# Element-wise sums moved from GpSimd to VectorE, and a gentler packing rule for buffers

## The chip, the cores and the metric

The kernel runs on one core of a Trainium2 chip. The metric is the device time of one execution in microseconds (us), the median of three runs. The engines have short names: PE is TensorE, DVE is VectorE, ACT is ScalarE, POOL is GpSimd and SP is SyncE, which only issues DMAs here.

## The reference, cut to what matters

One step of a diffusion backbone of one layer, over 2048 latent tokens on a grid of rows of 64 and 128 context tokens, with 1024 channels:

```python
hp, hs = modulate(xp, ...), modulate(xs, ...)          # context, latent
yp, sp_f, sp_b = hgrn2_mixer(hp, w_in, ..., zeros, zeros)
ys, _, _ = hgrn2_mixer(hs, w_in, ..., state[:, 0], state[:, 1])
xp, xs = xp + mod_p[2] * yp, xs + mod_s[2] * ys
hp, hs = modulate(xp, ...), modulate(xs, ...)
xp = xp + mod_p[5] * conv_ffn(hp, w_up, conv_w, conv_b, w_down, None)
xs = xs + mod_s[5] * conv_ffn(hs, w_up, conv_w, conv_b, w_down, 2)
return rms_norm(xp), rms_norm(xs), states

def conv_ffn(h, w_up, conv_w, conv_b, w_down, grid_axis):
    a, g = split(h @ w_up, 2)          # 2 x 2816 columns
    a = token_conv(a, conv_w, conv_b, grid_axis)   # three taps along the tokens
    return (silu(a) * g) @ w_down
```

## The kernel before, in words

All matrix products run on PE in f16 pairs: each operand is split into a high half (a cast on ACT) and a low half (the rest, by a subtraction on DVE), and three products are added up.

The first stage (to about 1210 us) is the recurrent mixer with its eight heads. Then come the output projection and the second norm (to about 1430 us), the up projection of the feed-forward block with convolution and gate (to about 2340 us), and the down projection with the final norm.

**The up projection.** The 22 blocks of 128 columns are taken in 11 pairs (`cb`), and for each pair the latent tokens in four pieces of 512 (`up(cb, p)`). One piece is a 2 by 2 block product done with seven block products, in Winograd's form, in the order 1, 2, 6, 5, 7, 3, 4 of the table `PROD`. It is done for two matrices at once (the convolved half `a` and the gate half `g`), so a product has 24 matmuls. Products 1, 6, 7 and 4 of one matrix use the same PSUM bank "A", products 5 and 3 the bank "C", and product 2 the bank "B". After products 1, 6, 5 and 4 ACT copies the bank to the buffer `c` (L1083, L1087, L1089, L1095). After 2, 7 and 3 DVE adds the bank to it (L1080). A bank that is used again must have been read first. For example, product 6 waits for the copy L1083 of product 1, with product 2 in between, and product 4 waits for the addition of product 7, with product 3 in between.

**The weights.** A product of this form needs, beside the four blocks of a weight matrix, four sums of them. `quad(cb, i)` makes them for one matrix: it loads two raw tiles of 512 KB (L1041, on SP's queue), yields once, forms s1 to s4 on POOL (L1046 to L1049), and then casts and splits eight blocks one by one (`part`, L1035 on ACT and L1036 on DVE). There are 22 quads, two for each pair.

**The gate.** `gate(cb, p)` takes a finished piece through the convolution (L1101 on ACT, L1108 and L1110 on DVE), Silu (L1135), the product with the gate half (L1137 on DVE), the sums and splits for the down projection (L1145 to L1149, L968 on ACT, L969 on DVE), and writes it to HBM (L1156). The context's 128 tokens go another way: `up_ctx` multiplies them plainly at the second piece (L414 to L416), and `gate_ctx` does convolution, Silu (L1177), the product with the gate half on POOL (L1179) and the split, once for each block, 22 times.

**What sets the order.** `quad`, `gate` and `gate_ctx` are generators. Behind each product `post()` takes one step of the oldest gate and two steps of the oldest entry of `pending`, in which the two gates of the context stand ahead of the two quads of the next pair. So the program's order has the sums directly behind the load of their raw tiles. When the program is built, a scheduler of the framework settles in which order each engine runs its instructions; an engine then runs them strictly in that order, each waiting for its semaphores. DMAs other than instruction loads are issued from SP alone.

**The placement.** Most SBUF buffers are placed by `place()`, which knows at which instruction each is born and last used. It gives each buffer, one by one, the place whose neighbours in time are farthest, up to a cap: `far` (600 instructions at first) or, for buffers that live over `AGE` instructions, `NEAR` (40). When a buffer finds no place, its lifetime goes into the list `tight`, it moves to the front of the order, and all is placed anew. When the list grows beyond `TRIES`, the search begins again with the next smaller `far` (300, 200, 100, 50, 20). Two buffers that share a place are tied by a wait: the first write of the later one waits for the last use of the earlier one.

Of the kernel before, what the change touches and what calls it, by code (L numbers as in the profile page):

```python
# [14 lines left out]
ALU = mybir.AluOpType  # L15
# [83 lines left out]
NEVER = 1 << 60  # L99
AGE = 400  # L100
NEAR = 40
TRIES = 60


def nbytes(shape, dt):
# [3 lines left out]
def place(tiles, far):  # L109

    at = [0] * len(tiles)
    for grain, lo, hi, some in (
            (TINY, 0, TINIES, [i for i, t in enumerate(tiles) if t.size <= 256]),
            (GRAIN, TINIES, ARENA, [i for i, t in enumerate(tiles) if t.size > 256])):
        slots = (hi - lo) // grain
        size = lambda i: -(-tiles[i].size // grain)  # L120
        age = lambda i: tiles[i].last - tiles[i].born
        some.sort(key=lambda i: (age(i) < NEVER // 2, size(i) != 11, age(i) <= AGE,
                                 -min(size(i), 16), tiles[i].born))
        tight = []
        while True:
            lives = [[] for _ in range(slots)]
            bad = None
            for i in some:
                t, n = tiles[i], size(i)
                cap = far  # L130
                if n == 11 or any(t.born <= b and a <= t.last for a, b in tight):
                    cap = 1
                elif age(i) > AGE:
                    cap = NEAR
                room = []
                for lv in lives:
                    j = bisect.bisect(lv, (t.born, 0))
                    before = t.born - lv[j - 1][1] + 1 if j else NEVER
                    after = lv[j][0] - t.last + 1 if j < len(lv) else NEVER
                    room.append(min(before, after, cap))  # L140
                best, where = 0, -1
                for st in (1 if n < 2 or n > 8 else 2 if n < 3 else 4, 1):
                    for s in range(0, slots - n + 1, st):
                        if room[s] > best:
                            g = min(room[s : s + n])
                            if g > best:
                                best, where = g, s
                                if g == cap:
                                    break
                    if where >= 0:  # L150
                        break
                if where < 0:
                    bad = i
                    break
                for lv in lives[where : where + n]:
                    bisect.insort(lv, (t.born, t.last))
                at[i] = lo + where * grain
            if bad is None:
                break
            if len(tight) > TRIES:  # L160
                return None
            tight.append((tiles[bad].born, tiles[bad].last))
            some.remove(bad)
            some.insert(0, bad)
    return at
# [3 lines left out]
def backbone_kernel(ctx: ExitStack, tc: tile.TileContext, **io):  # L169
# [20 lines left out]
    for t in keep:  # L190
        t.last = NEVER
    at = next(a for a in (place(tiles, far) for far in (600, 300, 200, 100, 50, 20)) if a)
    arena = ctx.enter_context(nc.sbuf_tensor([P, ARENA // 4], F32))
    base = int(arena.addr) if hasattr(arena, "addr") else BASE
# [18 lines left out]
def stages(nc, tl, pt, drt, xT, adaH, adaT, pvec, w_in, w_out, w_up, w_down, state, yT, st_out):  # L213
    V = nc.vector
    A = nc.scalar
    T = nc.tensor
    G = nc.gpsimd
# [664 lines left out]
    for hd in range(HEADS):  # L882
        for p in range(CTX):
            for part in range(2):
                i = hd * NSEG + 2 * p + part
# [80 lines left out]
    def split(dst, src, scale=None):  # L966

        A.activation(dst[0], src, AF.Copy)  # L968
        V.tensor_tensor(dst[1], src, dst[0], ALU.subtract)  # L969
# [58 lines left out]
    def quad(cb, i):  # L1028

        w = {}  # L1030
        WQ[cb, i] = w

        def part(z, src):
            t = w[z] = tl([P, 2, 512], F16, "w7")
            A.activation(t[:, 0], src, AF.Copy, scale=WS)  # L1035
            V.scalar_tensor_tensor(t[:, 1], src, WS, t[:, 0], ALU.mult, ALU.subtract)  # L1036

        raw = []
        for j in range(2):
            raw.append(tl([P, D], F32, "r"))  # L1040
            nc.sync.dma_start(raw[j], w_up[cb + j, i])  # L1041
        yield
        a11, a12, a21, a22 = (raw[j][:, 512 * k : 512 * k + 512]
                              for j in range(2) for k in range(2))
        s1, s2, s3, s4 = (tl([P, 512], F32, "s") for _ in range(4))
        G.tensor_tensor(s1, a21, a22, ALU.add)  # L1046
        G.tensor_tensor(s2, s1, a11, ALU.subtract)
        G.tensor_tensor(s3, a11, a21, ALU.subtract)
        G.tensor_tensor(s4, a12, s2, ALU.subtract)  # L1049
        yield  # L1050
        for z, src in (("A11", a11), ("A12", a12), ("A22", a22), ("A21", a21), ("S1", s1),
                       ("S2", s2), ("S3", s3), ("S4", s4)):
            part(z, src)
            yield
# [42 lines left out]
    def conv(cols, p, n):  # L1097


        for cb, y, a in cols:  # L1100
            A.activation(y, a, AF.Identity, bias=pv[:, PV_CB + cb : PV_CB + cb + 1],  # L1101
                         scale=cws[:, 22 + cb : 23 + cb])
        yield
        row = ROW if p != CTX else n
        for cb, y, a in cols:
            y3 = y.rearrange("p (r c) -> p r c", c=row)
            a3 = a.rearrange("p (r c) -> p r c", c=row)
            V.scalar_tensor_tensor(y3[:, :, 1:], a3[:, :, : row - 1], cws[:, cb : cb + 1],  # L1108
                                   y3[:, :, 1:], ALU.mult, ALU.add)
            V.scalar_tensor_tensor(y3[:, :, : row - 1], a3[:, :, 1:], cws[:, 44 + cb : 45 + cb],  # L1110
                                   y3[:, :, : row - 1], ALU.mult, ALU.add)
        yield
# [60 lines left out]
    def gate_ctx(cb, a, g):  # L1173
        n = NCTX
        y = tl([P, n], F32, "y")
        yield from conv([(cb, y, a)], CTX, n)
        A.activation(y, y, AF.Silu)  # L1177
        yield
        G.tensor_tensor(y, y, g, ALU.mult)  # L1179
        u = tl([P, 2, n], F16, "u")  # L1180
        yield
        split((u[:, 0], u[:, 1]), y)
        nc.sync.dma_start(UC[:, cb], u)

    def up_ctx(cb):
        n = NCTX
        for j in range(2):
            pa, pg = pt([P, 512], "pj"), pt([P, 512], "pj")
            for pp, i in ((pa, 0), (pg, 1)):
                for k in range(KT):  # L1190
                    wt = WQ[cb, i][("A11", "A12", "A21", "A22")[2 * j + k // 4]]
                    ks = slice(k % 4 * P, k % 4 * P + P)
                    mm3(pp[:, :n], (wt[:, 0, ks], wt[:, 1, ks]), TT[CTX][:, :, k], n,
                        k == 0, k == KT - 1)
            a, g = tl([P, n], F32, "y"), tl([P, n], F32, "y")
            A.activation(a, pa[:, :n], AF.Copy)
            A.activation(g, pg[:, :n], AF.Copy, scale=IWS)
            pending.append(gate_ctx(cb + j, a, g))
            post()
# [141 lines left out]
    for m in range(KT):  # L1341
# [8 lines left out]
        if m == 5:  # L1350
            load_og(3, ALL)
            load_res(3)
            load_og(CTX, ALL)
            load_res(CTX)
    pending.extend([quad(0, 0), quad(0, 1)])
    for m in range(KT):
        project(3, ALL, (m,))
# [9 lines left out]
    for cb in range(0, NCB, 2):  # L1367
        last = cb + 2 == NCB
        for p in range(CTX):
            up(cb, p)  # L1370
            if p == 1:
                up_ctx(cb)
                if not last:
                    pending.extend([quad(cb + 2, 0), quad(cb + 2, 1)])
            if last and p < 2:
                pending.append(blocks_down(p))
            if last and p == 2:
                while pending:
                    post()
                load_uc()  # L1380
                for j in range(2):
                    load_xd(CTX, j, 0, NCTX)
# [76 lines left out]
```

## Time and profile before

| | |
|---|---|
| median of three runs | 2852.59 us (2851.67 to 2853.03) |
| profiled execution | 2852.6 us |
| its span, first to last instruction | 2850.8 us |
| PE busy | 2722.7 us, 96% |
| DVE busy | 1885.1 us, 66% |
| ACT busy | 1076.9 us, 38% |
| POOL busy | 279.7 us, 10% |

"Busy" is the time in which an engine executes. PE's weight loads run beside its matmuls and are counted apart. Matmuls are pipelined, so their ends are modelled. An idle stretch ahead of an instruction is put down to what released it. Where an instruction waited for several semaphores, the one named is the one that came last by the profile. Times of a position in the run are counted from the first instruction.

### The profile page before, as it was taken

The numbers are of one execution on the slowest core, as the hardware profiler recorded it, in microseconds if no ns is written. First come the engines' busy times: TensorE is split into PE (matmuls) and PEld (weight loads), VectorE is DVE, ScalarE is ACT, GpSimd is POOL, SyncE is SP. The second block draws the span as 40 slices with busy tenths as digits, with TensorE's granted clock in tenths as the row PEclk, the third lists the DMA queues.
The fourth block names the chain that finished last, engine by engine and source line by source line (L and its number), as shares of the span: only waits on it lengthen the run. The fifth ranks groups of instructions, "written<-read, shape, count | busy, mean of one in ns | idle before, by whom it ended". The sixth has DMA issues, their size and how long they took to land. (4 is left out here: it accounts for less than half of the span.)

```text
span 2850.8 us, 57278 instructions
## 1 busy us (share of the span) xinstructions
PE 2722.7 (96%) x23576; PEld 2136.0 (75%) x23576; DVE 1885.1 (66%) x5198; ACT 1076.9 (38%) x2373; POOL 279.7 (10%) x210
## 2 busy tenths in 40 slices
PE   8999999999999999999999999999999978999998
PEld 4666767677777777754588888888889867788887
DVE  7877878778876667746996666666666777233132
ACT  5433333343433333424564545454454534001001
POOL 0100000000000000000221111111110234000000
PEclk9999999999999999999999999999999999999999
DMA  7101211030201010435112122222221344343342
GB/s 265 43 30 44 74 53 63 24 101 24 72 16 43 9 51 15 148 111 180 53 58 84 56 83 71 69 71 71 84 69 55 112 120 143 121 149 132 124 154 78
DMA packets 188310, 236.86 MB, mean 83 GB/s; under 512 B 12304, under 2 KB 142736, under 8 KB 188048
## 3 DMA queue, kind: packets, MB, share of 16 engines
q1 hardware_dynamic: 188048, 233.19, 25.8%
q8 instruction: 185, 3.03, 0.5%
q14 instruction: 77, 0.63, 0.1%
HBM read 163.55 MB, written 69.60 MB: 82 GB/s over the span
## 5 line engine op out<-in xcount | busy, mean ns | idle before, releaser
L1074 PEld LDWEIGHTS <-w 128*128 128x128 f16 x7392 | 728.8, 99 | 148.3 <-issue 58.6
L1074 PE MATMUL pj_p<-T,w 128*128 128x256 f16 x4224 | 498.0, 276 | 50.6 <-ACT c L1083 33.7
L1292 PEld LDWEIGHTS <-wd 128*128 128x128 f16 x3696 | 363.8, 99 | 70.7 <-issue 17.1
L1292 PE MATMUL pj_p<-U,wd 128*128 128x256 f16 x3168 | 358.0, 274 | 14.8 <-DVE x L1301 12.3
L1074 PE MATMUL sc_p<-T,w 128*128 128x256 f16 x3168 | 369.5, 273 | 2.8 <-ACT c L1089 2.8
L414 PE MATMUL pj_p<-H,wp 128*128 128x512 f16 x768 | 290.8, 380 | 2.7 <-ACT H L393 2.4
L415 PE MATMUL pj_p<-H,wp 128*128 128x512 f16 x768 | 292.2, 380 | 0.6 <-DVE H L398 0.5
L416 PE MATMUL pj_p<-H,wp 128*128 128x512 f16 x768 | 292.0, 380 | 0.0
L536 PE MATMUL pj_p<-wp,H 128*128 128x256 f16 x1024 | 279.9, 273 | 0.0
L537 PE MATMUL pj_p<-wp,H 128*128 128x256 f16 x1024 | 279.9, 273 | 0.0
L538 PE MATMUL pj_p<-wp,H 128*128 128x256 f16 x1024 | 279.9, 273 | 0.0
L1301 DVE SCALAR_TENSOR_TENSOR x<-pj_p,g,x 128x256 f32<-128x256 f32 x96 | 46.3, 483 | 224.4 <-PE pj_p L1292 220.8
L416 PEld LDWEIGHTS <-wp 128*128 128x128 f16 x960 | 94.2, 98 | 91.2 <-issue 2.4
L414 PEld LDWEIGHTS <-wp 128*128 128x128 f16 x960 | 94.2, 98 | 83.2 <-issue 3.3
L415 PEld LDWEIGHTS <-wp 128*128 128x128 f16 x960 | 94.2, 98 | 80.7 <-issue 1.7
L746 POOL TENSOR_TENSOR rs<-rs,mh 128x4 f32<-128x4 f32 (+1 forms) x40 | 41.6, 1040 | 1071.6 <-DVE rs L744 988.1
L416 PE MATMUL pj_p<-og,wo 128*128 128x512 f16 (+1 forms) x320 | 109.0, 351 | 3.7 <-DVE wo L411 3.7
L1101 ACT ACTIVATE y<-c,pv,cws 128x512 f32<-128x512 f32 x88 | 71.3, 812 | 108.9 <-DVE c L1080 93.4
L1108 DVE SCALAR_TENSOR_TENSOR y<-c,cws,y 128x504 f32<-128x504 f32 x88 | 76.1, 867 | 50.8 <-ACT y L1101 50.5
L538 PEld LDWEIGHTS <-H 128*128 128x128 f16 x1024 | 100.5, 98 | 12.1
L537 PEld LDWEIGHTS <-H 128*128 128x128 f16 x1024 | 100.5, 98 | 12.0
L536 PEld LDWEIGHTS <-H 128*128 128x128 f16 x1024 | 100.6, 98 | 11.8
(281 smaller groups left out, 5180.1 us busy)
## 6 DMA issues: line engine op xcount, KB each, us to landing
ud<-u SPq DMA_DIRECT2D x44, 896.0 KB, 4.8
U<-ud SPq DMA_DIRECT2D x56, 704.0 KB, 4.4
r<-w_up SPq DMA_DIRECT2D x44, 512.0 KB, 3.7
wr<-w_in SPq DMA_DIRECT2D x40, 512.0 KB, 4.2
wr<-adaT SPq DMA_DIRECT2D x32, 512.0 KB, 3.6
rawd<-w_down SPq DMA_DIRECT2D x16, 704.0 KB, 7.2
x<-xT SPq DMA_DIRECT2D x32, 256.0 KB, 5.4
sp<-oT SPq DMA_DIRECT2D x32, 256.0 KB, 3.4
```

The lines of the kernel that those rows point to most:

```text
L414: T.matmul(out, whl[0], hhl[:, 0, :n], start=first, stop=False)
L415: T.matmul(out, whl[0], hhl[:, 1, :n], start=False, stop=False)
L416: T.matmul(out, whl[1], hhl[:, 0, :n], start=False, stop=last)
L536: T.matmul(o, hp[k][:, 0, tok], wvg[0][:, k], start=(k == 0), stop=False)
L537: T.matmul(o, hp[k][:, 0, tok], wvg[1][:, k], start=False, stop=False)
L538: T.matmul(o, hp[k][:, 1, tok], wvg[0][:, k], start=False, stop=(k == KT - 1))
L746: G.tensor_tensor(r2[:, :nb], r[:, :nb], mh[:, :nb], ALU.pow)
L1074: T.matmul(out, wt[:, a, ks], tt[:, b, k], start=first and k == 0 and n == 0, stop=i in (2, 3, 4) and k == 3 and n == 2, skip_group_check= ...
L1101: A.activation(y, a, AF.Identity, bias=pv[:, PV_CB + cb : PV_CB + cb + 1], scale=cws[:, 22 + cb : 23 + cb])
L1108: V.scalar_tensor_tensor(y3[:, :, 1:], a3[:, :, : row - 1], cws[:, cb : cb + 1], y3[:, :, 1:], ALU.mult, ALU.add)
L1292: T.matmul(out, w[:, a, k], UT[p, zb][b][:, k], start=first and i % 2 == 0 and k == 0 and q == 0, stop=n in (2, 3, 4) and k == KP - 1 and ...
L1301: V.scalar_tensor_tensor(x, get(src), g64[:, 1, m, 0:1], x, ALU.mult, ALU.add)
```

## The change

Three things are changed. The four sums of a quad are issued on VectorE and no more on GpSimd. So is the product of the context's gate. In the placement a buffer whose life touches a spot in `tight` had its cap set to 1 at once; now the cap is halved once for each such spot that it touches, down to 1 at the least, and 120 spots may be tried instead of 60. Buffers of eleven grains keep the cap 1.

```diff
-TRIES = 60
+TRIES = 120
...
                 t, n = tiles[i], size(i)
-                cap = far
-                if n == 11 or any(t.born <= b and a <= t.last for a, b in tight):
+                cap = NEAR if age(i) > AGE else far
+                for a, b in tight:
+                    if t.born <= b and a <= t.last:
+                        cap >>= 1
+                if n == 11:
                     cap = 1
-                elif age(i) > AGE:
-                    cap = NEAR
+                cap = max(cap, 1)
...
-        G.tensor_tensor(s1, a21, a22, ALU.add)
-        G.tensor_tensor(s2, s1, a11, ALU.subtract)
-        G.tensor_tensor(s3, a11, a21, ALU.subtract)
-        G.tensor_tensor(s4, a12, s2, ALU.subtract)
+        V.tensor_tensor(s1, a21, a22, ALU.add)
+        V.tensor_tensor(s2, s1, a11, ALU.subtract)
+        V.tensor_tensor(s3, a11, a21, ALU.subtract)
+        V.tensor_tensor(s4, a12, s2, ALU.subtract)
...
         A.activation(y, y, AF.Silu)
         yield
-        G.tensor_tensor(y, y, g, ALU.mult)
+        V.tensor_tensor(y, y, g, ALU.mult)
```

## Rows read from the trace of the kernel before

**Rows 1.** The page's first part: busy us, share of the span, instructions.

```profile
PE 2722.7 (96%) x23576; PEld 2136.0 (75%) x23576; DVE 1885.1 (66%) x5198; ACT 1076.9 (38%) x2373; POOL 279.7 (10%) x210
```

**Rows 2.** Busy time by stretch; us: PE, PEld, DVE, ACT, POOL, clock, DMA.

```profile
1340.00:1500.00 160.00, 150.60 (x1228) 110.76 (x1227) 148.24 (x218) 96.82 (x170) 35.44 (x22) 0.97 0.17 56
1500.00:2260.00 760.00, 730.18 (x7047) 654.72 (x7045) 503.82 (x901) 372.17 (x786) 119.51 (x90) 0.99 0.24 73
2260.00:2460.00 200.00, 160.57 (x1657) 141.02 (x1655) 137.61 (x153) 76.46 (x110) 60.00 (x19) 0.92 0.45 133
```

**Rows 3.** PE's waits, 1500 to 2260: total us, times, longest us.

```profile
PE pj_p L1074 <- ACT c L1083: 23.3, 11, 2.8
PE sc_p L1074 <- ACT c L1089: 2.5, 2, 1.9
```

**Rows 4.** The chain of waits, 2046.5 to 2056: start us, us, what.

```profile
2046.57 2.85 POOL s L1048
2049.42 0.42 POOL y L1179
...
2050.09 1.13 ACT w L1035 x2
2051.22 0.28 ACT c L1083
...
2053.01 2.62 PE sc_p L1074 x24
```

**Rows 5.** Instruction groups of POOL, 1500 to 2260: busy us, mean ns, idle before.

```profile
L1048 POOL TENSOR_TENSOR s<-r,r 128x512 f32<-128x512 f32 x18 | 34.6, 1923 | 67.4 <-DMA r<-w_up 54.5 <-DVE u L969 12.9
L1049 POOL TENSOR_TENSOR s<-r,s 128x512 f32<-128x512 f32 x18 | 27.2, 1509 | 2.8 <-DVE u L969 2.1
L1047 POOL TENSOR_TENSOR s<-s,r 128x512 f32<-128x512 f32 x18 | 25.2, 1398 | 45.6 <-issue 43.9 <-DVE w L1036 1.5
L1046 POOL TENSOR_TENSOR s<-r 128x512 f32<-128x512 f32 x18 | 23.8, 1324 | 438.3 <-DMA ud<-u 299.7 <-DMA r<-w_up 61.1 <-DVE y L1110 59.6
L1179 POOL TENSOR_TENSOR y<-y,y 128x128 f32<-128x128 f32 x18 | 10.1, 564 | 79.6 <-ACT y L1177 77.4 <-ACT y L1197 2.1
```

**Rows 6.** Single lines of DVE, whole run: ns minimum/median/maximum, first and last start.

```profile
L362 DVE TENSOR_TENSOR s<-s,s x35: 281/682/1764, 1316.5 to 1420.2; 128x512 f32<-128x512 f32 x28, 128x128 f32<-128x128 f32 x7
L1108 DVE SCALAR_TENSOR_TENSOR y<-c,cws,y x88: 728/743/3622, 1449.8 to 2357.0; 128x504 f32<-128x504 f32 x88
L1036 DVE SCALAR_TENSOR_TENSOR w<-r,w x88: 674/683/1761, 1370.8 to 2241.5; 128x512 f16<-128x512 f32 x88
L1145 DVE TENSOR_TENSOR t<-y x44: 412/424/1514, 1456.5 to 2362.4; 128x256 f32<-128x256 f32 x44
L1080 DVE SCALAR_TENSOR_TENSOR c<-sc_p,c x176: 407/418/425, 1426.2 to 2351.4; 128x256 f32<-128x256 f32 x176
```

**Rows 7.** PE's waits, 1340 to 1500.

```profile
PE pj_p L1074 <- ACT c L1087: 2.5, 1, 2.5
```

**Rows 8.** Instruction groups of DVE, 1500 to 2260.

```profile
L1108 DVE SCALAR_TENSOR_TENSOR y<-c,cws,y 128x504 f32<-128x504 f32 x74 | 61.0, 826 | 42.3 <-ACT y L1101 42.0
...
L1036 DVE SCALAR_TENSOR_TENSOR w<-r,w 128x512 f16<-128x512 f32 x72 | 54.4, 772 | 17.5 <-ACT w L1035 17.1
...
L1145 DVE TENSOR_TENSOR t<-y 128x256 f32<-128x256 f32 x38 | 23.6, 621 | 0.6
```

**Rows 9.** The page's DMA issues: count, KB each, us to landing.

```profile
r<-w_up SPq DMA_DIRECT2D x44, 512.0 KB, 3.7
```

**Rows 10.** ACT's waits, 1500 to 2260.

```profile
ACT w L1035 <- DMA r<-w_up: 24.8, 9, 6.9
```

**Rows 11.** SP's waits, 1500 to 2260.

```profile
SPq L1041 <- DVE y L1110: 64.2, 6, 11.1
```

**Rows 12.** PE's waits, 2260 to 2460.

```profile
PE pj_p L1292 <- DVE x L1301: 8.0, 3, 4.7
PE sc_p L1292 <- DMA U<-ud: 4.2, 1, 4.2
```

## The prediction

> **What bounds the kernel now.** I read the page's busy line first: TensorE (PE) is busy 2722.7 of the 2850.8 us span, so no change of this kind can give back more than the 128 us in which PE stands still, and the change touches only part of those [rows 1]. Next, busy time by stage, to see where the stillness is: 9.4 us in 1340 to 1500 (the first two weight quads are built there), 29.8 us in 1500 to 2260 (the nine middle column pairs of the up projection), 39.4 us in 2260 to 2460 (the passage to the down projection). In the first of these VectorE (DVE) is busy 148.2 of 160 us, in the second only 503.8 of 760 [rows 2]. Third, PE's waits in the middle stretch: 23.3 of the 29.8 us are one wait, 11 times, for ScalarE's copy `c` at L1083, which empties product 1 so that product 6 may reuse its bank [rows 3]. Fourth, the chain of waits around one of those gaps. The reader is to see in it that Pool's sum s3 (L1048) runs 2.85 us, the context's gate product (L1179) stands behind it on Pool, ScalarE's split waits for that product, and the PE-releasing copy L1083 comes behind the split and two weight casts on ScalarE's queue [rows 4]. So the stall of each column pair is a Pool queue seen through ScalarE's queue.
>
> **The change part by part.** My base is the profiled execution: 2852.6 us, its span of 2850.8 and 1.8 us around it. The median of the three runs is 2852.59, the same to 0.1 us.
>
> *Part 1, the recurring gap.* The change takes L1048 and L1179 off Pool. In the chain the two take 2.85 + 0.42 = 3.27 us between the moment the inputs are there and the moment ScalarE may go on [rows 4]. Their means over the stretch, 1.92 and 0.56 us, say that this instance of the sum is one of the long ones [rows 5]. On VectorE the trace shows a 128x512 two-input f32 operation at a median of 682 ns and the 128x128 form of the same line at 281 ns, the minimum of that row [rows 6]. At worst the product stands behind two sums there: 2 x 0.68 + 0.28 = 1.64 us. The copy then comes 3.27 - 1.64 = 1.63 us earlier. Over 11 gaps of 23.3 / 11 = 2.1 us that is 17.9 us. I take 17, because the shorter gaps can't give back more than they are. Bounds: 0, if another operation of the same queue is as late, and 23.3, if nothing is.
>
> *Part 2, quads that are late as a whole.* At the first and the last quads PE waits for ScalarE behind all four sums: 2.5 us at L1087 in 1340 to 1500 and 2.5 us at L1089 [rows 3, 7]. Four sums cost Pool 1.32 + 1.40 + 1.92 + 1.51 = 6.15 us at their means [rows 5], and VectorE 4 x 0.68 = 2.7. That is 3.4 us earlier, which is longer than either gap. I take 4 of the 5.0 us; bounds 0 and 5.
>
> *Part 3, what VectorE has to carry.* In the middle stretch it gets 18 quads x 4 x 0.68 + 18 products x 0.28 = 54 us. But it also loses time: its operations with two operands in SBUF are stretched when Pool runs. L1108 has a median of 743 ns and a maximum of 3622, L1145 424 and 1514, while L1080, which reads one operand from PSUM, stays within 407 to 425 [rows 6]. With the means of this stretch, (826 - 743) x 74 + (772 - 683) x 72 + (621 - 424) x 38 ns = 6.1 + 6.4 + 7.5 = 20 us go away in three groups alone [rows 6, 8]. Net +34 us on an engine with 256 us idle: VectorE goes from 66% to at most 71% there and stays no bound, so I cost this at nothing. The cover is thin in 1340 to 1500. There 16 sums and 2 products are 11.4 us more, against 11.8 us of idle time less what the stretching gives back [rows 2]. If the cover fails, all 11 us lie on the way to the first up products. I take +2, nearer to the relief than to full cost; bounds 0 and 11.
>
> The Trainium skill speaks against this part: Perfetto Trace Analysis, Optimizing Scalar/DVE Operations, says that offloading to GPSIMD may make sense where DVE is saturated, though it adds that the two share a read port and moving work between them might not help. By its first half the sum would get the full 11 us at the saturated stretch; by its second half, and by the stretched rows, close to nothing. The rows side with the second half here.
>
> *Part 4, a new wait on VectorE.* The sums read the raw weights straight behind their load, and a load lands 3.7 us after its issue [rows 9]. On Pool a wait for it blocked only other sums and the context's product. On VectorE it blocks the `c` additions (L1080), for which product 4 waits, and the convolution. How the instructions are ordered on VectorE is settled when the program is built, so the trace of before can't show the wait; the nearest row is ScalarE's, which waited for the same loads 9 times, 24.8 us in all, longest 6.9 [rows 10]. Between the product that needs the addition (7) and the one that needs its result (4) lies one product, 2.62 us [rows 4]. A mean wait of 2.76 us is all but hidden (9 x 0.14 = 1.3 us); the longest exposes 4.3 us, at 9 places 38 us. I take +4, near the row's mean. Below nothing isn't excluded either, since a sum that starts sooner frees the raw buffers sooner; I give that 3 us.
>
> *Part 5, the placement.* Buffers near a spot that did not fit were packed with no distance at all to the last use of their place; now their distance is halved per failed spot. Such waits are in the trace: loads of raw weights (L1041) were held 64.2 us on SyncE for convolution operations (L1110) that do not compute anything they need [rows 11]. More distance makes them shorter, but every address can change, so stages that the edit does not name may move both ways. The trace can't price it. The passage 2260 to 2460, where PE idles 39.4 us on transfers, gates and buffers, is where most could move [rows 2, 12]. I take 0, with -20 (half of that passage) and +25 (the middle stretch's or the passage's idle time again, in good part) as bounds.
>
> Sum: -17 - 4 + 2 + 4 + 0 = -15 us, 2852.6 - 15 = 2837.6, so 2838.
>
> **The rivals.**
> 1. *The gap is refilled (no change).* ScalarE still has two weight casts, 1.13 us, ahead of the copy [rows 4], and they wait for sums that now stand in VectorE's queue. If the sums come last there, the copy is as late as before, and only part 2 is won against parts 3 and 4: about 2850. For: the chain is dense on ScalarE and VectorE ahead of Pool's 2.85 us. Against: the work between is 1.6 us shorter.
> 2. *VectorE stands at a load (slower).* Place: the first sum of a quad, just behind its load. Price: if at each of the 18 middle quads it waits as long as the longest row of ScalarE, 4.3 us exposed each, 77 us; at half the quads 38. Against the 19 us that parts 1, 2 and 3 win, it decides from 19 / 18 = 1.1 us exposed a quad, a wait of 3.7 us, which is a whole load. With the wait exposed at half the quads: 2852.6 - 19 + 38 = 2872. For: order by program puts the sum right behind the load. Against: ScalarE in the same position waited at only 9 of them.
> 3. *The new placement is worse (slower or same).* The search ends only when everything fits, else it begins again with all distances smaller; then buffers that rotated freely come to wait. With 25 us of new waits: 2862.
> 4. *The placement gives on top of the sum.* Half of the passage's idle time: about 2818.
>
> That the edit doesn't do what it says is part of rival 3 for the placement; the operations surely move.
>
> **How the numbers follow.** Forecast (2824 to 2847) 0.48; rival 1 0.15; rival 2 0.10; rival 3 0.12; rival 4 0.15. A measurement of this kernel tells 0.2%, 5.7 us, from no change. Faster by more than that: forecast and rival 4, 0.63. Within it: rival 1 and an edge of rival 3, 0.16. Slower: the rest, 0.21. The range, for 8 in 10, takes in rivals 1 and 4, and rival 3 to its centre: 2812 to 2864; the forecast's own range is 2824 to 2847.
>
> **What would show it.** Part 1: PE's wait for L1083 in the middle stretch falls from 23.3 us to some 6, and Pool has left the chain there. Part 2: no 2.5 us gaps at the first and last quads. Part 3: L1108's and L1036's means close to 743 and 683 ns; sums at 0.68 us, products at 0.28. Part 4: a row of VectorE waiting for the load `r`, under 25 us in all, and few PE waits for L1080. Part 5: PE's idle time in 0 to 1340 and behind 2260 about as before. Wrong it would be if PE's idle time in 1500 to 2260 stays above 25 us (rival 1), if VectorE's waits for `r` pass 60 us (rival 2), or if the main difference lies outside 1340 to 2260 (rivals 3 and 4).

## The result, and the profile after

The changed kernel takes 2810.63 us in the median (four runs, 2808.24 to 2815.83), the kernel before 2852.64. The ratio is 0.9856, with an interval of 0.9839 to 0.9873: 42 us faster. The forecast was 15 us, 2838, with a range of 2812 to 2864. The direction was right, the size was not, and the time lies just below the range.

The profiled execution has a span of 2806.1 us, 44.7 less than before. All lines of the changed kernel behind the placement are numbered two higher: L1074 is L1076, L1083 is L1085, and so on. First the busy line of its page, which answers to [rows 1]:

```profile
PE 2707.9 (97%) x23576; PEld 2129.9 (76%) x23576; DVE 1896.1 (68%) x5308; ACT 1068.8 (38%) x2373; POOL 131.8 (5%) x100
```

PE does the same 23576 matmuls in 14.8 us less, and stands still 98.2 us instead of 128.1, which is 29.9 less. Both numbers add up to the 44.7.

Next, busy time by stage, cut at the same work in both kernels: the end of the mixer's last projection, the first up product, the first product of the eleventh column pair, the third product of the down projection, the end. Columns as in [rows 2]. The kernel before:

```profile
0.00:1201.60 1201.60, 1176.31 (x9572) 833.02 (x9573) 914.84 (x3485) 460.96 (x1135) 53.57 (x65) 0.99 0.20 62
1201.60:1409.00 207.40, 203.72 (x1246) 111.11 (x1245) 144.67 (x297) 81.41 (x162) 21.88 (x16) 0.98 0.36 122
1409.00:2249.90 840.90, 801.68 (x7704) 717.23 (x7702) 579.16 (x1016) 424.07 (x887) 138.68 (x102) 0.99 0.23 70
2249.90:2438.40 188.50, 150.35 (x1566) 132.16 (x1565) 135.05 (x150) 77.81 (x117) 60.00 (x19) 0.92 0.45 132
2438.40:2850.80 412.40, 390.67 (x3498) 342.44 (x3497) 111.33 (x254) 32.66 (x76) 5.58 (x8) 0.99 0.39 128
```

The changed kernel:

```profile
0.00:1185.90 1185.90, 1171.37 (x9572) 830.35 (x9573) 918.97 (x3499) 459.36 (x1136) 52.19 (x65) 1.00 0.19 63
1185.90:1391.20 205.30, 202.63 (x1247) 111.02 (x1245) 143.65 (x289) 82.65 (x163) 10.48 (x8) 0.99 0.37 127
1391.20:2204.20 813.00, 794.72 (x7705) 713.98 (x7703) 584.46 (x1121) 418.83 (x884) 3.33 (x2) 1.00 0.25 73
2204.20:2398.50 194.30, 150.79 (x1567) 131.98 (x1565) 137.42 (x148) 77.42 (x117) 60.26 (x17) 0.90 0.44 128
2398.50:2806.10 407.60, 388.41 (x3498) 342.59 (x3495) 111.62 (x254) 30.51 (x76) 5.58 (x8) 0.99 0.39 129
```

The third column is the length. The mixer is 15.7 us shorter, the first ten column pairs 27.9, the output projection and norms 2.1, the last stage 4.8; the passage is 5.8 us longer. So a third of the gain lies in a stage in which no engine was changed.

PE's waits in the first ten pairs of the changed kernel, which answer to [rows 3, 7]:

```profile
PE pj_p L1076 <- DVE c L1082: 9.6, 10, 2.5
PE pj_p L1076 <- ACT c L1085: 5.5, 4, 3.2
...
PE sc_p L1076 <- ACT c L1091: 0.2, 1, 0.2
```

The recurring wait for the copy of product 1 is gone but for four places, 23.3 to 5.5 us. A new one stands in its place, for VectorE's additions. Single lines of VectorE, as in [rows 6] (minimum/median/maximum in ns), and its waits at the sums, 1480 to 2204 (total us, times, longest):

```profile
L1048 DVE TENSOR_TENSOR s<-r x22: 679/690/694, 1348.6 to 2192.7; 128x512 f32<-128x512 f32 x22
L1038 DVE SCALAR_TENSOR_TENSOR w<-r,w x88: 676/683/693, 1355.3 to 2197.2; 128x512 f16<-128x512 f32 x88
L1147 DVE TENSOR_TENSOR t<-y x44: 411/420/426, 1436.3 to 2313.6; 128x256 f32<-128x256 f32 x44
L1082 DVE SCALAR_TENSOR_TENSOR c<-sc_p,c x176: 411/417/425, 1405.0 to 2305.1; 128x256 f32<-128x256 f32 x176
L1181 DVE TENSOR_TENSOR y<-y,y x22: 281/285/293, 1443.0 to 2262.9; 128x128 f32<-128x128 f32 x22
```

```profile
DVE s L1049 <- DMA r<-w_up: 18.0, 7, 4.3
DVE s L1048 <- DMA r<-w_up: 16.7, 5, 5.3
...
DVE s L1050 <- DMA ud<-u: 7.0, 2, 3.5
```

The maxima of L1036 (1761) and L1145 (1514) have fallen to 693 and 426 ns. The maximum of the convolution has not: 3622 ns before, 3633 now. The price of the sums and of the product is what the prediction took.

### The profile page after: what moved, and what is told of

Its sections match the earlier page's. It is cut to its first block, busy times and chain, and to the rows that moved or that the text cites. A ratio compares the mean times of both kernels' runs of the same rounds, so it can differ in the third digit from the quotient of the medians.

```text
span 2806.1 us, 57255 instructions
## 1 busy us (share of the span) xinstructions
PE 2707.9 (97%) x23576; PEld 2129.9 (76%) x23576; DVE 1896.1 (68%) x5308; ACT 1068.8 (38%) x2373; POOL 131.8 (5%) x100
## 4 chain that ended last, share of the span: by engine, by line
PE 72%; DVE 15%; DMA 5%; ACT 3%; issue 2%; POOL 0%; SPq 0%; DVEq 0%; POOLq 0%; ACTq 0%
PE pj_p L1076 11%; PE pj_p L1294 10%; PE sc_p L1076 8%; PE pj_p L417 7%; PE pj_p L418 7%; PE pj_p L416 7%; PE pj_p L540 4%; PE pj_p L538 4%; PE pj_p L539 4%; PE sc_p L692 2%; PE sc_p L1294 2%; DMA ud<-u 2%; DMA r<-w_up 1%; PE sc_p L652 1%; PE sc_p L661 1%
## 5 line engine op out<-in xcount | busy, mean ns | idle before, releaser
L1076 PEld LDWEIGHTS <-w 128*128 128x128 f16 x7392 | 725.3, 98 | 126.0 <-issue 40.0
L1076 PE MATMUL pj_p<-T,w 128*128 128x256 f16 x4224 | 491.4, 274 | 33.8 <-DVE c L1082 10.4
L1294 PE MATMUL pj_p<-U,wd 128*128 128x256 f16 x3168 | 358.5, 274 | 21.4 <-DVE x L1303 11.7
L1076 PE MATMUL sc_p<-T,w 128*128 128x256 f16 x3168 | 369.2, 273 | 1.6 <-ACT c L1091 1.6
L1303 DVE SCALAR_TENSOR_TENSOR x<-pj_p,g,x 128x256 f32<-128x256 f32 x96 | 46.3, 483 | 231.9 <-PE pj_p L1294 227.5
L363 ACT ACTIVATE n<-x 128x256 f32<-128x256 f32 (+1 forms) x63 | 23.4, 398 | 277.2 <-DVE x L1303 225.2
L511 ACT ACTIVATE f<-pj_p 128x512 f32<-128x512 f32 x64 | 38.1, 597 | 196.4 <-PE pj_p L418 196.4
L540 PEld LDWEIGHTS <-H 128*128 128x128 f16 x1024 | 100.2, 98 | 11.9
L539 PEld LDWEIGHTS <-H 128*128 128x128 f16 x1024 | 100.2, 98 | 11.8
```

The lines of the kernel that those rows point to most:

```text
L511: A.activation(ft, pj[:, :n], AF.Tanh, scale=0.5 * IWS)
L539: T.matmul(o, hp[k][:, 0, tok], wvg[1][:, k], start=False, stop=False)
L540: T.matmul(o, hp[k][:, 1, tok], wvg[0][:, k], start=False, stop=(k == KT - 1))
L1076: T.matmul(out, wt[:, a, ks], tt[:, b, k], start=first and k == 0 and n == 0, stop=i in (2, 3, 4) and k == 3 and n == 2, skip_group_check= ...
L1294: T.matmul(out, w[:, a, k], UT[p, zb][b][:, k], start=first and i % 2 == 0 and k == 0 and q == 0, stop=n in (2, 3, 4) and k == KP - 1 and ...
L1303: V.scalar_tensor_tensor(x, get(src), g64[:, 1, m, 0:1], x, ALU.mult, ALU.add)
```

## The experiments

Where medians are compared, the kernel before ran on the same chip (medians 2849.7 to 2853.4). The lengths of stages are from the profiles, one execution each, cut as above. The changed kernel's four times lie up to 7.6 us apart, so differences of a few us in a length tell little.

| kernel | us, median | ratio to before | mixer | first ten pairs | passage |
|---|---|---|---|---|---|
| before | 2852.6 | 1 | 1201.6 | 840.9 | 188.5 |
| changed | 2810.6 | 0.9856 | 1185.9 | 813.0 | 194.3 |
| e1 packing only | 2837.2 | 0.9950 (0.9937 to 0.9963) | 1186.5 | 837.8 | 194.4 |
| e2 engines only | 2825.0 | 0.9907 (0.9892 to 0.9923) | 1202.1 | 815.2 | 186.7 |
| e3 sums only | 2838.1 | 0.9955 (0.9941 to 0.9969) | 1203.4 | 823.8 | 188.4 |
| e4 product only | 2856.9 | 1.0016 (1.0007 to 1.0025) | 1202.3 | 844.3 | 188.8 |
| e5 packing in the mixer only | 2834.5 | 0.9945 (0.9929 to 0.9962) | 1189.6 | 833.7 | 188.8 |
| e7 changed, and the down sums on VectorE | 2793.0 | 0.9797 (0.9781 to 0.9814) | 1185.3 | 811.5 | 181.5 |

**e1 and e2, the two halves of the change.** e1 is the changed kernel with the five operations back on Pool:

```diff
-        V.tensor_tensor(s1, a21, a22, ALU.add)
+        G.tensor_tensor(s1, a21, a22, ALU.add)
...
-        V.tensor_tensor(y, y, g, ALU.mult)
+        G.tensor_tensor(y, y, g, ALU.mult)
```

> The changed kernel with the four sums and the context's product back on Pool: only the packing rule is new, and every buffer has the address that it has in the changed kernel. Theory A (two separate gains: the packing shortens the mixer, the engines shorten the up projection): the mixer is about 1186 us long as in the changed kernel, the up projection's first ten pairs stay near 841 us, total about 2852.6 - 16 - 2 = 2835 (2828 to 2842). Rival B (the packing alone does nearly all, since it also takes away the waits in the up projection): total under 2818 and PE's wait for L1085 (the copy of product 1) in the up projection well under 10 us. Rival C (the scheduler's new order after the move of the sums makes the mixer's gain): the mixer stays at 1201 us.

e2 is the kernel before with these five lines on VectorE and nothing else changed.

> The kernel before with the four sums and the context's product on VectorE and nothing else: the old packing rule and the old addresses. Theory A: mixer 1201 to 1202 us as before, the first ten pairs of the up projection near 815 us instead of 841, total about 2852.6 - 26 = 2827 (2820 to 2836), PE's wait for L1083 there under 6 us. Rival B: under 8 us of gain, over 2845, since VectorE then waits for the old neighbours. Rival C: the mixer falls to about 1186 us.

Measured: e1 is 15.0 us faster than before, e2 27.2, together 42.2; the whole change gave 42. The product of the ratios, 0.9950 x 0.9907 = 0.9857, agrees with the ratio of the whole, 0.9856. So the halves add up, theory A holds on both sides, and rivals B and C fall: the mixer is 1186.5 us with the packing alone and 1202.1 without it. PE's waits in the up projection, e1 (1400 to 2240):

```profile
PE pj_p L1076 <- ACT c L1085: 28.5, 17, 2.7
```

and e2 (1410 to 2225.3):

```profile
PE pj_p L1074 <- DVE c L1080: 11.9, 11, 2.1
PE pj_p L1074 <- ACT c L1083: 2.4, 4, 1.6
...
PE sc_p L366 <- DVE s L362: 1.0, 1, 1.0
PE sc_p L1074 <- ACT c L1089: 0.5, 1, 0.5
```

The new packing alone does nothing for the recurring wait. The move alone removes nearly all of it. Of the packing's two edits only the halved cap counts: with 60 spots instead of 120, `place()` gives the changed kernel the same addresses.

**e3 and e4, the two moves apart.** e3 moves only the four sums of the kernel before, e4 only the product:

```diff
-        G.tensor_tensor(y, y, g, ALU.mult)
+        V.tensor_tensor(y, y, g, ALU.mult)
```

> The kernel before with only the four sums on VectorE; the context's product stays on Pool, old addresses. By the prediction's part 1 the stall is the product's place behind a sum on Pool's queue, so with the sums gone the product runs at once: theory A expects nearly the whole of the gain of the two moves together (within 4 us of it). Rival D (the product itself on Pool, 0.56 us and its semaphores, is what ScalarE waits for): under half of it.

> The kernel before with only the context's product on VectorE; the sums stay on Pool, old addresses. By part 1 ScalarE's split no longer waits for Pool, but the two weight casts ahead of the copy still wait for the sums (ScalarE waited 19.0 us for L1046) and VectorE's operations are still stretched. Theory A: a third to a half of the recurring gap goes, 6 to 12 us with what follows from it, 2840 to 2847. Rival D: as much as both moves together. L1108's mean stays near 826 ns in the up projection, since Pool's sums still run.

Measured: e3 gains 14.1 us, e4 loses 4.7. Together they gain 27.2, so these two do not add up, and both expectations missed. ScalarE's waits for Pool, first the longest of the kernel before (1400 to 2300), then two of e4 (1400 to 2240):

```profile
ACT u L968 <- POOL y L1179: 23.6, 20, 2.5
```

```profile
ACT w L1035 <- POOL s L1046: 19.9, 9, 3.9
ACT w L1035 <- POOL s L1048: 19.0, 8, 3.1
```

and e3, first PE's waits for the additions and for the copy of product 1, then ScalarE's for Pool:

```profile
PE pj_p L1074 <- DVE c L1080: 16.1, 11, 2.3
PE pj_p L1074 <- ACT c L1083: 6.0, 7, 1.6
```

```profile
ACT u L968 <- POOL y L1179: 11.9, 20, 1.3
```

With the product alone gone, ScalarE waits at the next thing that Pool owes it, the sums: for L1048 it had waited 1.8 us before and waits 19.0 now. PE's wait for L1083 stays at 23.7 us there, and its idle time in the ten pairs is about that of before (38.7 us against 39.2); what e4 lost there is busy time, 805.6 us against 801.7 at a mean granted clock of 0.98 instead of 0.99. With the sums alone gone, PE's wait for L1083 falls to 6.0 us, so most of that wait was theirs. The product still costs ScalarE 11.9 us in 20 waits though no sum stands ahead of it on Pool (it runs 893 ns there in the median, 502 before), and PE waits longer for the additions than in e2. The chain of [rows 4] named two Pool instructions; either one alone keeps ScalarE's queue waiting.

**e5, e8, e9 and e10: is it distance?** e5 keeps all engines as before and applies the new rule only to buffers born in the mixer, which has the program's instructions up to 14000:

```diff
                 for a, b in tight:
                     if t.born <= b and a <= t.last:
-                        cap >>= 1
+                        cap = cap >> 1 if t.born < MIXER else 1
```

> The kernel before, all sums on Pool, with the gentler packing rule for buffers born in the mixer only; every later buffer keeps the address of before. Theory E (distance: what a buffer's first write waits for is the last use of its place, and close neighbours make PE wait): the mixer falls from 1201.6 to 1186 to 1188 us, everything behind it stays, total 2837 to 2840. Rival F (the gain sits in the norms, the up projection or the last stage, and the mixer only looked shorter in one execution): the mixer stays within 4 us of 1201 and the total above 2848.

The other three keep the old rule and change only from which end some buffers of the mixer search their place, e8 the capped ones (`cap == 1`), e9 the others (`cap != 1`), e10 those of one grain (`n == 1`):

```diff
-                    for s in range(0, slots - n + 1, st):
+                    spots = range(0, slots - n + 1, st)
+                    for s in spots[::-1] if t.born < MIXER and cap == 1 else spots:
```

> The kernel before with the old rule (cap 1 at once), but in the mixer a capped buffer searches its place from the other end. The search then ends only at the cap 100, and in the mixer no buffer is placed 5 or fewer instructions behind the last use of its place and 9 are 6 to 20 behind (before: 57 and 51; changed kernel: 0 and 12). Theory E: mixer 1184 to 1190 us although the rule is the old one. Rival G (the gain belongs to the new rule's order or to lucky addresses, not to distance): mixer 1198 to 1206 us.

> The kernel before with the old rule, uncapped buffers of the mixer searching from the other end. Now 250 buffers of the mixer stand 5 or fewer instructions behind the last use of their place and 244 are 6 to 20 behind. Theory E: the mixer gets longer than before in proportion, by 20 us or more (over 1222). Rival G: 1186 to 1206, no more than the lottery of addresses.

> The kernel before with the old rule, buffers of one grain of the mixer searching from the other end: other addresses, and nearly the same number of close neighbours as before (75 within 5 instructions, 63 at 6 to 20). Theory E: mixer 1198 to 1208 us, near before. Rival G: as likely at 1186 as at 1201, or far off both.

Measured: e8 2835.3 us, e9 2922.9, e10 2848.7, one execution each. The addresses behind the mixer change in them as well: of the 950 buffers born there, 126 keep theirs in e8, 244 in e9 and 140 in e10. So theory E is read from the mixer alone.

The table counts, from the addresses and lifetimes of `place()`, the mixer's buffers that were born few instructions behind the last use of their place. Beside it stand PE's idle time behind the first 160 us (length less busy time of that stretch) and the mixer's length:

| kernel | within 5 | 6 to 20 | PE idle, 160 us to the mixer's end | mixer |
|---|---|---|---|---|
| changed | 0 | 12 | 1.4 | 1185.9 |
| e8 | 0 | 9 | 1.3 | 1196.8 |
| e5 | 1 | 20 | 2.4 | 1189.6 |
| before | 57 | 51 | 9.1 | 1201.6 |
| e10 | 75 | 63 | 10.7 | 1204.4 |
| e9 | 250 | 244 | 48.6 | 1263.2 |

The stretches for the changed kernel, before, e8 and e9, in this order:

```profile
160.00:1185.90 1025.90, 1024.52 (x8636) 743.69 (x8635) 788.61 (x3137) 379.06 (x988) 37.11 (x38) 1.00 0.17 52
```

```profile
160.00:1201.60 1041.60, 1032.51 (x8689) 748.37 (x8688) 784.41 (x3120) 381.87 (x991) 38.27 (x38) 1.00 0.16 51
```

```profile
0.00:160.00 160.00, 141.62 (x860) 83.00 (x861) 126.25 (x343) 76.66 (x141) 14.63 (x27) 0.95 0.36 127
160.00:1196.80 1036.80, 1035.50 (x8714) 750.40 (x8713) 784.53 (x3122) 379.37 (x990) 37.12 (x38) 1.00 0.15 49
```

```profile
160.00:1263.20 1103.20, 1054.62 (x8622) 747.73 (x8620) 795.84 (x3162) 383.34 (x983) 35.35 (x37) 0.99 0.15 48
```

Idle time behind 160 us follows the number of close neighbours under either rule, so the gain there is distance and not the rule's own order (theory E). e9 and e10 came out as theory E had them. But that gain is only half of the mixer's 15.7 us: 7.7 us (9.1 to 1.4). Another 3.1 are idle time in the first 160 us and 4.9 are busy time of PE, and these runs do not show that distance made them.

e8 missed its number all the same. Its mixer is 1196.8 and not 1184 to 1190 us, because PE idles 18.4 us in the first 160; there the changed kernel idles 13.2 and e9, with the most close neighbours, 11.8. What sets the order of that start was not found. e8 also gained more than its mixer shows. Its first ten pairs take 821.3 us instead of 840.9, and PE's wait there for the copy of product 1 is 14.5 us instead of 23.3, with all sums on Pool; its passage is 12.4 us longer (200.9). So addresses can shorten the recurring wait too, though those of the changed kernel do not (28.5 us in e1). Which addresses do it was not found.

e5 was as forecast in the mixer within 2 us. Behind it, it gained 8 us more, 6.5 of them in the first column pair (95.3 to 88.8 us). There PE's wait of 5.0 us for the norm's sums (L362) is gone, with every sum still on Pool; 2.3 us remain at the same matmul, with no releaser that the profile shows. The addresses behind the mixer are not quite those of before: 21 of the 950 buffers have others, all of them buffers `s` born around the first two quads. Whether these made the difference is not shown.

How one close neighbour costs time can be followed in the kernel before. SyncE's row of waits (395 to 426), VectorE's instructions and PE's:

```profile
SPq L321 <- DVE qb L631: 11.4, 1, 11.4
```

```profile
422.23 1.23 DVE L324 SCALAR_TENSOR_TENSOR og<-wr,wp 128x1024 f16<-128x1024 f32 x1 [1.72 <-DMA wr<-adaT]
423.38 0.08 DVE L324 DVE_READ_ACCUMULATOR og<-wr,wp 128x1 f32 x1
423.38 0.69 DVE L796 TENSOR_TENSOR op<-sc_p,op 128x512 f32<-128x512 f32 x1
```

```profile
424.12 0.66 PE L659 MATMUL sc_p<-I,k 128*128 128x128 f32 x4 [1.97 <-DVE op L796]
```

The load of a modulation weight is held 11.4 us until an operation of the recurrence (L631) is through with its place, whose last use stands 2 instructions ahead of the load in the program. It lands 1.7 us after VectorE has come to the operation that needs it, the addition L796 stands behind that, and PE waits 1.97 us. The load computes nothing with that operation's data; they share an address.

**e6, later sums.** In the changed kernel, the four sums two steps later:

```diff
+        for z, src in (("A11", a11), ("A12", a12)):
+            part(z, src)
+            yield
         s1, s2, s3, s4 = (tl([P, 512], F32, "s") for _ in range(4))
```

> The changed kernel with the four sums of a quad issued two steps later, behind the casts and splits of A11 and A12, so that their load has more time to land before VectorE reaches them. Theory H (in the changed kernel PE's waits for VectorE's additions, 9.9 us in 11 between 1400 and 2240, come from VectorE standing at a sum whose load has not landed, 44 us in all): VectorE's waits for the load at the sums fall under 15 us, PE's waits for L1082 (the additions) there under 4 us, total 6 to 10 us below the changed kernel. Rival I (the scheduler had put the sums as late as their data allows, and the wait only moves to the split of A11 or to ScalarE's cast): total within 4 us of the changed kernel. Caution: the buffers are born elsewhere, so addresses change as well; the mixer's length is read apart.

Measured: 2831.25 us, ratio 0.9934 (0.9919 to 0.9949), about 21 us above the changed kernel. Neither theory had this price. VectorE's wait for the load stayed (33.9 us at the first sum, 10.1 at the second). ScalarE's grew from 23.2 to 113.5 us (1480 to 2220): the cast of A11, and no longer a sum, is the first to read the load, and rival I had that place. More loads also came late for a store, by SyncE's row:

```profile
SPq L1043 <- DMA ud<-u: 72.1, 18, 5.1
```

That row had 37.6 us in 9 waits in the changed kernel. The edit moved the births of the buffers, and raw loads got places that a store of the gate still had to leave. This is not the whole account: all of SyncE's waits at these loads together fell, from 210.6 to 140.2 us. Other addresses changed as well; 4 of the 21 us lie in the mixer (1190.0 us).

**e7, the down projection's sums as well.** In the changed kernel:

```diff
-        G.tensor_tensor(a22, a21, a22, ALU.add)
+        V.tensor_tensor(a22, a21, a22, ALU.add)
...
-        G.tensor_tensor(a12, a12, a11, ALU.subtract)
+        V.tensor_tensor(a12, a12, a11, ALU.subtract)
```

> The changed kernel with the 16 sums of the down projection's weights (128x1408, on Pool 3.4 to 4.0 us each, 58 us in all) on VectorE as well; same addresses. Theory J (what stretches VectorE's two-operand work in the passage, up to 3.6 us for a 0.74 us convolution step, is Pool running beside it): no operation of the convolution over 1.0 us any more, the sums some 1.6 to 1.9 us each, 28 us more on VectorE, which is busy 137 of 194 us there; PE's longest gap of the passage (8.8 us) shrinks by half, total 5 to 12 us below the changed kernel. Rival K (VectorE becomes late there, since 28 us more stand in its queue ahead of splits that PE waits for): total 3 us or more above the changed kernel.

Measured: 2792.98 us (2791.70 to 2793.57), better than both kernels; 0.9797 against 0.9856 is 0.6%, some 17 us below the changed kernel, more than the 5 to 12 expected. Of the 14.3 us between the two profiled spans 12.8 lie in the passage, which went from 194.3 to 181.5 us. VectorE and Pool in the changed kernel, around its longest gap of 8.8 us (in e7 the longest in the up products of that pair is 3.5; the longest of the whole passage did not shrink by half, it is now another, 10.2 us for VectorE's L1303, 4.9 in the changed kernel):

```profile
2283.09 3.63 DVE L1110 SCALAR_TENSOR_TENSOR y<-c,cws,y 128x504 f32<-128x504 f32 x1
2286.65 7.18 DVE L1112 SCALAR_TENSOR_TENSOR y<-c,cws,y 128x504 f32<-128x504 f32 x2
```

```profile
2282.71 3.48 POOL L1237 TENSOR_TENSOR rawd<-rawd,rawd 128x1408 f32<-128x1408 f32 x1
2286.27 3.48 POOL L1238 TENSOR_TENSOR rawd<-rawd,rawd 128x1408 f32<-128x1408 f32 x1
2289.82 3.47 POOL L1239 TENSOR_TENSOR rawd<-rawd,rawd 128x1408 f32<-128x1408 f32 x1
```

and the same convolution line and one of the sums in e7 (2200 to 2400):

```profile
L1110 DVE SCALAR_TENSOR_TENSOR y<-c,cws,y 128x504 f32<-128x504 f32 x10 | 7.4, 740 | 4.8 <-ACT y L1103 4.8
...
L1239 DVE TENSOR_TENSOR rawd<-rawd,rawd 128x1408 f32<-128x1408 f32 x4 | 6.5, 1616 | 0.0
```

Each convolution step ends some 0.5 us after a Pool sum does. Three steps of 0.74 us took 10.8. The sum itself takes 1.62 us on VectorE and 3.48 on Pool. VectorE's busy time in the passage falls from 137.4 to 125.5 us though it does 16 sums more.

**e11 and e12, more distance for transfers.** Both are e7 with other lifetimes for the search:

```diff
+    for tag, t in marked:
+        if tag == "u":
+            t.last += 60
```

(e12: `if tag == "r": t.born -= 60`.)

> The kernel of e7_down_sums (all sums on VectorE, new rule) whose placement takes each buffer u of the gate, which a store of 896 KB reads last, as living 60 instructions longer, so that whoever gets its place comes later. Theory L (distance counted in instructions is too short where the last use is a transfer: in the changed kernel SyncE held raw loads 37.6 us and VectorE's sums 7.0 us for these stores): waits for the store fall to under 10 us on SyncE, PE's waits for the additions L1082 from 10 to under 6 us, total 3 to 8 us below e7. Rival M (the room is taken from others: distances elsewhere shrink, 61 spots did not fit instead of 51): total within 4 us of e7 or above it.

> The kernel of e7_down_sums whose placement takes each raw weight buffer r as born 60 instructions earlier than its load is written in the program, so that the last use of its place lies 60 instructions farther back. Theory L: SyncE's waits at the raw loads (210 us in 34 waits in the changed kernel, 108 of them for convolution steps) fall by more than half, VectorE's waits at the sums fall from 44 to under 20 us, total 3 to 10 us below e7. Rival M: 80 spots did not fit, the mixer's or the gate's buffers come closer, total within 4 us of e7 or above it.

Measured: 2798.39 us (ratio 0.9807, 0.9791 to 0.9822) and 2802.67 (0.9828, 0.9812 to 0.9844). Theory L fails in both. SyncE's raw loads still wait 39.3 us for stores in e11, and 207.6 us in all in e12, near the 210 of the changed kernel. VectorE's waits for transfers at the sums fall only from 44 to 35 and 37 us, PE's for the additions grow to 13.4 and 19.2 us. e11 can't be told from e7; e12 is some 9 us above it by the ratios. In e11 the passage is 13.8 us shorter than in e7 (167.7) and the ten pairs are 11.7 longer (823.2), so one stage lost what the other won; which of the new addresses did it is open.

## Why the prediction was wrong

**The step that failed first is part 5, the placement, taken at 0.** e1 measures it at -15.0 us. The prediction looked for PE's idle time only in 1340 to 2460, and gave the mixer no term, though the diff touched a search that places all its buffers. PE's idle time in the mixer was 25.3 us (1201.60 - 1176.31) and is 13.4 in e1, and its busy time is 3.2 us less. Of the idle time the part behind the first 160 us is shown to come from close neighbours; the cause of the rest is open. The lower bound of -20 took in the size, but it was read from the passage. The rivals too had the placement only at the passage, which in fact got 5.9 us longer in e1 (188.5 to 194.4).

**Parts 1 to 4, -15 together, measured -27.2 in e2.** In the first ten pairs of e2 PE's idle time fell by 21.5 us (39.2 to 17.8) and its busy time by 4.2. Two waits of the kernel before that the forecast did not weigh, beside those of [rows 3, 7]:

```profile
PE sc_p L366 <- DVE s L362: 5.0, 1, 5.0
...
PE pj_p L1074 <- DVE c L1080: 1.9, 3, 1.0
```

By PE's waits in the first ten pairs:

- *Part 1* (17): the wait for L1083 fell from 23.3 to 2.4 us, 21. The place was right, the size nearly. The prediction took both Pool instructions off and was right in that. Its price put the cost on the product's turn behind a sum on Pool's queue, and this was only part of it: the sums alone bring the wait to 6.0 us (e3), the product alone brings nothing (e4), because ScalarE waits for the sums as well.
- *Part 2* (4 of 5): L1089 fell from 2.5 to 0.5 and all of L1087, 4.0 us in 3 waits of which the forecast had counted 2.5, is gone. Right, and a little more.
- *Part 3* (+2): wrong in sign. PE's wait for the norm's sums, L362, was 5.0 us before and is 1.0 in e2. It is 1.0 in e3 too and 4.9 in e4, so at the old addresses the sums did it; with other addresses it is gone without them too (e1 and e5, where 2.5 and 2.3 us with no releaser named remain at the same matmul). VectorE's busy time in the stretch of the norms rose by only 2.8 us (144.7 to 147.5), though 8 of the sums moved to it there, 5.5 us at 0.69. The rule of the Trainium skill that was weighed there (Perfetto Trace Analysis, Optimizing Scalar/DVE Operations) would have made this term worse; its remark on the shared port fits the runs better.
- *Part 4* (+4): the wait came where it was put. In e2 VectorE stood at the sums for their loads 41.0 us in 13 waits, and 20.9 us more for stores that still held a place. PE's wait for the additions went from 1.9 to 11.9 us: +10. The term was under-sized, and neither later sums (e6) nor more distance (e11, e12) took the wait away.
- *Left out: the clock.* In e2 PE's busy time in the ten pairs falls from 801.7 to 797.4 us for the same products. Behind some of the gaps the granted clock was 0.50, which is 1.2 instead of 2.4 GHz. Busy time and clock of the kernel before, in three stretches behind the gap at 424 (the clock is the third number from the end):

```profile
424.20:425.30 1.10, 1.10 (x11) 1.02 (x12) 1.10 (x3) 0.49 (x1) 0.00 (x0) 1.00 0.00 0
425.30:428.70 3.40, 3.40 (x19) 2.42 (x17) 3.40 (x16) 1.14 (x2) 0.00 (x0) 0.50 0.51 133
428.70:432.10 3.40, 3.40 (x33) 3.05 (x32) 3.40 (x18) 1.28 (x8) 0.00 (x0) 1.00 0.55 153
```

PE idled 1.97 us ahead of it, and then got through 19 matmuls in 3.4 us, against 33 in the next 3.4 at full clock. Over the whole run the change gave back 14.8 us of PE's busy time, and the mean granted clock rose from 0.986 to 0.990. An estimate from these means, 0.014 x 2850.8 - 0.010 x 2806.1 us, puts some 12 of the 14.8 to the clock. The prediction counted gaps and never what follows them.

Of the rivals, 4 (the placement gives on top) came true, with 0.15 and in another stage than the one that its price was read from. That its price, some 20 us, is near the 15 of e1 is luck.

## What to carry to other kernels

When a diff touches an allocator, give every stage that it places for a term of its own, and look at how many buffers stand close behind the last use of their place: an engine that runs in order turns one held load into a wait of others. When two instructions of a slow engine stand in one queue, moving one of them may gain half (e3) or nothing (e4). A gap of the bounding engine costs its length and, where the clock falls behind it, some more; count both.

## What was not expected of the hardware

A Pool operation beside VectorE did not slow it by a share here, it held it up while it ran. Convolution steps of 0.74 us took 3.5 to 3.6 us beside Pool sums of 3.48, one step for each sum, while additions with one operand in PSUM stayed at 411 to 425 ns in the same kernel. The Trainium skill, SBUF — State Buffer, in SBUF: two separate sides, states that the port pair which the two engines share is locked for a whole instruction and the other side blocks. The timeline of the changed kernel agrees. So work moved from Pool to VectorE can make VectorE less busy: 137.4 to 125.5 us in the passage of e7.
